# The tail of a hybrid encoder block: the last expert's down weights by columns, and the last norm's mean and offset added on PE

## The chip, the cores and the metric

The kernel runs on one core of one Trainium2 chip. The metric is the device time of one execution in microseconds (us), the median of three runs. TensorE is called PE, VectorE DVE, ScalarE ACT, GpSimd POOL, and SyncE, whose queue issues most DMAs, SP.

## The reference

One encoder layer over 256 tokens of width 1024 in float32: a projection, a sparse and a banded attention, a merge, a layer norm, and then the part that matters here, a mixture of 32 experts of which every token uses four, and a last layer norm.

```
for each expert e:   h = (clip(x @ w_up + b_up) + 1) * swish(min(x @ w_gate + b_gate, 7))
                     y = h @ w_down[e] + b_down[e]
ffn[t] = sum over the token's four experts of gate * y
z = alpha * x + ffn
out = (z - mean(z)) * rsqrt(var(z) + 1e-5) * ln2_g + ln2_b
```

## The kernel before

All 32 experts are run, each on up to 64 gathered tokens, so their weights are streamed once: per expert four loads of 2 MB ("gu", gate and up weights) and two of 2 MB ("d", down weights). A load goes into one of 13 slots of 2 MB; `plan` writes down the order (gate and up of expert e + 1, then down of expert e), `pump` issues on SP's queue as many loads as slots are free, and `take` hands a landed one to PE. SP works through its queue in program order, and a load waits there for an earlier one to land or for its slot.

The loop over experts has this order of the work: gate and up products of e on PE (`run_gate_up`, lines 782 and 784), the copy of the two results to the tile `work["gu"]` on ACT (`evac_gu`, through `acopy`, line 176), the down product of expert e - 1 (`run_down`, line 816) and its copy, and `act_fn`: transposes on PE (line 799), then some six DVE operations and one ACT operation for each half (lines 803 to 809). After every second expert `combine` (line 828) multiplies the down results by the routing weights and adds them to four PSUM banks, `sums[tb][n]` (two blocks of 128 tokens, two halves of 512 columns), which hold alpha * x from the start. At the end of iteration 26 the 32 down biases are loaded into the single tile "bd" (line 984), and at the end of iteration 28 they are added by PE. All order is written by hand: every engine does its instructions in the order of the program.

Behind the loop the last expert, 31, has a tail of its own. Its gate and up products are copied and activated, then expert 30's down product runs, then its own. Its down weights come as four pieces of 1 MB, by halves of the columns and halves of the contraction. `down_half` (line 1007) multiplies a piece in products of 256 columns, 64 partitions each, `combine_half` (line 1014) adds to the sums, and `bn_stats` (line 1016) reads each bank. The gain and offset of the last norm come in one row of 8 KB behind the last weights (line 994) and are spread to all partitions by POOL (line 995). The norm then runs per token block: block 0 on DVE, with two passes per half (subtract the mean and multiply by the gain, multiply by the inverse deviation and add the offset), block 1 with one ACT pass (line 1036) and two more on POOL or DVE. Each of the four results of 128 x 512 is stored by a DMA of its own (lines 1040 to 1047).

Of the kernel before, what the change touches and what calls it, by code (L numbers as in the profile page):

```python
# [20 lines left out]
CAP = 64  # L21
OVERFLOW_AT = 20
BD_AT = 26
TOPK = 64
ALPHA = 2.0 ** 0.25
EPS = 1e-5
# [25 lines left out]
def body(nc, tc, slots, sm, psp, xT_d, x_d, w_g0, w_qi, w_in, ikgb_d, wuk_d,  # L52
# [12 lines left out]
    def two(name):  # L65

        t = slot(name)
        return t[:, 0:2048], t[:, 2048:4096]

    def one(name):  # L70

        return slots[1].tile([128, 2048], F32, name=name, tag="one")
# [4 lines left out]
    def bank(name):  # L77
        return psp.tile([128, 512], F32, name=name, tag="ps")
# [4 lines left out]
    def plan(key, src):  # L83
        pending.append((key, src))
# [12 lines left out]
    def take(key):  # L97
        while key not in loaded:
            load_next()
        return loaded[key]  # L100

    def both(src, i):
        return lambda t: [(t[:, h * 2048:(h + 1) * 2048], src[i + h]) for h in range(2)]
# [11 lines left out]

    def plan_d(e):
        for c in range(2):

            plan(("d", e, c), wd_d[e, c] if e < NE - 1 else both(wdl_d, 2 * c))

    plan_gu(0)
    for e in range(NE):
# [49 lines left out]
    def vcopy(o, i):  # L172
        V.tensor_copy(o, i)

    def acopy(o, i):
        A.activation(o, i, AF.Copy)  # L176
# [643 lines left out]
    def rows_of(e, p, first=0, size=512):  # L820

        r = slice(64 * (e % 2), 64 * (e % 2) + 64)
        for n in range(2):
            acopy(work["y"][r, first + n * size:first + (n + 1) * size], p[64 * n:64 * n + 64, 0:size])
# [98 lines left out]
    def down_biases(bd_s):  # L923

        gT = bd_s[0:NE, 1024:1024 + T]
        bd = bd_s[0:NE, 0:1024]
        p = bank("gT")
        for tb in range(NT):
            PE.transpose(p[0:NE, tb * 128:(tb + 1) * 128], gt[:, tb, :], ident)
        acopy(gT, p[0:NE, 0:256])  # L930
        for tb in range(NT):
            for n in range(2):
                summed(tb, n, gT[:, tb * 128:(tb + 1) * 128], bd[:, n * 512:(n + 1) * 512])

    def count():

        p = bank("cnt")
        for tb in range(NT):
            PE.matmul(p[:, 0:NE], tri[:, 1, :], selb[:, tb, :], start=(tb == 0), stop=(tb == 1))
        V.tensor_reduce(cnt, p[:, 0:NE], axis=AX.X, op=ALU.max)  # L940
        V.tensor_copy(cnti, cnt)
# [14 lines left out]
    for e in range(last):  # L956
        ps = run_gate_up(e)
        if e == 0:
            for gain, op in ((ln1[0], ALU.mult), (ln1[1], ALU.add)):
                V.tensor_tensor(x1, x1, gain[:, None, :].to_broadcast([128, NT, D]), op=op)  # L960
            open_work()
            gates()
        evac_gu(ps)
        if e == 0:
            open_sums()
        if e == 1:
            dispatch_weights(0)
        if e == 3:
            count()
        if e >= 1:  # L970
            run_down(e - 1)
        else:
            pump(0)
        if e % 2 == 1:
            dispatch(e // 2 + 1)
            dispatch_weights(e // 2 + 1)
        act_fn(work["hT"], bias_of(0, e), bias_of(1, e))
        if e >= 2 and e % 2 == 0:
            combine(e // 2 - 1)
        if e == OVERFLOW_AT:  # L980
            overflow(one("ov"))
        if e == BD_AT:
            bd_s = one("bd")
            SP.dma_start(bd_s[0:NE, 0:1024], bd_d)
        if e == BD_AT + 2:
            down_biases(bd_s)

    evac_gu(run_gate_up(last))
    hT = xg_rows(0, 4).rearrange("p j (a s) -> p (j a) s", a=2)
    act_fn(hT, bias_of(0, last), bias_of(1, last))  # L990
    run_down(last - 1)
    ln2_s, acc_s = two("ln2_acc")
    acc = acc_s.rearrange("p (b c) -> p b c", b=2)
    SP.dma_start(ln2_s[0:1, :], ln2_d)
    G.partition_broadcast(ln2_s, ln2_s[0:1, :])
    A.preload_act_table(AF.Sqrt)


    lng, lnb = ln2_s[:, 0:1024], ln2_s[:, 1024:2048]
    hs = [slice(h * 512, (h + 1) * 512) for h in range(2)]  # L1000
    yps = [bank("y"), bank("y")]

    def down_half(h, c2, js=range(4)):
        wd = take(("d", last, h)).rearrange("p (j f) -> p j f", j=KD)
        for j in js:
            for n in range(2):
                PE.matmul(yps[h][64 * n:64 * n + 64, 0:256], hT[:, 4 * c2 + j, :], wd[:, 4 * c2 + j, n * 256:(n + 1) * 256],  # L1007
                          start=(c2 + j == 0), stop=(c2 == 1 and j == 3), skip_group_check=True)
        if c2 == 1 and 3 in js:
            rows_of(last, yps[h], h * 512, 256)  # L1010

    def combine_half(h, tbs=range(NT)):
        for tb in tbs:
            PE.matmul(sums[tb][h], work["pt"][:, last // 2 % 2, tb, :], work["y"][:, h * 512:(h + 1) * 512],  # L1014
                      start=False, stop=True, skip_group_check=True)
            V.bn_stats(lnst[:, tb, h, :], sums[tb][h])  # L1016
            if h == 1:
                V.bn_aggr(lnmv[:, tb, 0:2], lnst[:, tb, 0:2])  # L1018

    down_half(0, 0)  # L1020
    down_half(0, 1)
    down_half(1, 0)
    down_half(1, 1, (0, 1))
    combine_half(0, (0,))
    down_half(1, 1, (2, 3))
    combine_half(0, (1,))
    combine_half(1)
    A.activation(lnmv[:, :, 2], lnmv[:, :, 1], AF.Sqrt, bias=epst[:, 0:1])
    m0, m1 = lnmv[:, 0, :], lnmv[:, 1, :]
    a0, a1 = acc[:, 0, :], acc[:, 1, :]  # L1030
    s0, s1 = sums
    V.scalar_tensor_tensor(a0[:, hs[0]], s0[0], m0[:, 0:1], lng[:, hs[0]], op0=ALU.subtract, op1=ALU.mult)  # L1032
    V.reciprocal(lnmv[:, :, 3], lnmv[:, :, 2])
    V.tensor_scalar(m1[:, 4:5], m1[:, 0:1], m1[:, 3:4], -1.0, op0=ALU.mult, op1=ALU.mult)  # L1034
    for h in (1, 0):
        A.activation(a1[:, hs[h]], s1[h], AF.Identity, bias=m1[:, 4:5], scale=m1[:, 3:4])
    G.tensor_tensor(a1[:, hs[1]], a1[:, hs[1]], lng[:, hs[1]], op=ALU.mult)
    G.tensor_tensor(a1[:, hs[1]], a1[:, hs[1]], lnb[:, hs[1]], op=ALU.add)
    V.scalar_tensor_tensor(a0[:, hs[0]], a0[:, hs[0]], m0[:, 3:4], lnb[:, hs[0]], op0=ALU.mult, op1=ALU.add)  # L1039
    SP.dma_start(out_d[0:128, hs[0]], a0[:, hs[0]])  # L1040
    V.scalar_tensor_tensor(a0[:, hs[1]], s0[1], m0[:, 0:1], lng[:, hs[1]], op0=ALU.subtract, op1=ALU.mult)  # L1041
    V.scalar_tensor_tensor(a0[:, hs[1]], a0[:, hs[1]], m0[:, 3:4], lnb[:, hs[1]], op0=ALU.mult, op1=ALU.add)  # L1042
    SP.dma_start(out_d[0:128, hs[1]], a0[:, hs[1]])
    A.dma_start(out_d[128:256, hs[1]], a1[:, hs[1]])
    V.tensor_tensor(a1[:, hs[0]], a1[:, hs[0]], lng[:, hs[0]], op=ALU.mult)  # L1045
    V.tensor_tensor(a1[:, hs[0]], a1[:, hs[0]], lnb[:, hs[0]], op=ALU.add)  # L1046
    SP.dma_start(out_d[128:256, hs[0]], a1[:, hs[0]])


# [62 lines left out]
```

## Time and profile before

| what | us |
|---|---|
| median of 3 runs | 1116.69 (1115.77 to 1116.75) |
| the profiled execution | 1116.79 |
| its span, first to last instruction | 1114.9 |
| PE busy / DVE / ACT / POOL | 1033.9 / 310.1 / 232.6 / 25.4 |
| granted PE clock, mean | 0.996 |
| HBM read | 435.48 MB, 392 GB/s over the span |

The span is what the trace shows; the rest of the execution's time lies around it. A busy share says nothing about what bounds a stage: matmuls are pipelined, and PE is counted as busy while a product drains. What ended an idle time is given behind an arrow as its releaser.

### The profile page before, as it was taken

The page shows a single profiled execution, that of the slowest core. Times are in us where ns is not written, and L with a number is a line of the kernel's source. Part 1 is how long each engine was busy: PE and PEld are TensorE (multiplying, and loading weights), DVE is VectorE, ACT ScalarE, POOL GpSimd, SP SyncE. Part 2 cuts the span into 40 slices and gives each one's busy share as a digit, 9 for nine tenths or more (in the row PEclk, how much of TensorE's full clock was granted, in tenths as well). Part 3 has the DMA queues.
Part 4 walks back from the last instruction along what each step waited for, and adds up shares of the span by engine and source line. Part 5 has one row for each costly group of instructions (what it writes and reads, how often), then busy time and mean ns, then how long its engine had stood idle before and what let it go on. Part 6 is the DMA issues. An engine that isn't in the chain of part 4 may idle for free. (4 is left out here: it accounts for less than half of the span.)

```text
span 1114.9 us, 13223 instructions
## 1 busy us (share of the span) xinstructions
PE 1033.9 (93%) x5559; PEld 524.8 (47%) x5559; DVE 310.1 (28%) x743; ACT 232.6 (21%) x433; POOL 25.4 (2%) x23
## 2 busy tenths in 40 slices
PE   8999999999999999988889988897998888889995
PEld 8999998443434344333343434342434343333432
DVE  5879667411111111211111111111111102011123
ACT  3647534211111111111111111111111111111112
POOL 0320000000000000000000000000000000000001
PEclk9999999999999999999999999999999999999999
DMA  9926649999999999999999999999999999999993
GB/s 365 386 77 265 263 170 398 395 424 427 427 427 429 426 429 427 429 427 426 429 427 428 427 428 427 428 427 426 427 427 428 426 427 430 425 411 429 427 424 147
DMA packets 34678, 437.44 MB, mean 392 GB/s; under 512 B 4116, under 2 KB 4884, under 8 KB 6324
## 3 DMA queue, kind: packets, MB, share of 16 engines
q1 hardware_dynamic: 34182, 435.46, 92.9%
q10 hardware_dynamic: 432, 1.08, 0.3%
q8 instruction: 45, 0.74, 0.3%
q14 instruction: 19, 0.16, 0.0%
HBM read 435.48 MB, written 1.05 MB: 392 GB/s over the span
## 5 line engine op out<-in xcount | busy, mean ns | idle before, releaser
L782 PE MATMUL gu<-ld,x_wa 128*64 128x512 f32 x1024 | 452.1, 596 | 15.7 <-DMA ld<-in_dram 12.0
L784 PE MATMUL gu<-ld,x_wa 128*64 128x512 f32 x1024 | 452.1, 596 | 0.0
L782 PEld LDWEIGHTS gu<-ld,x_wa 128*64 128x64 f32 x1024 | 136.3, 137 | 309.6 <-issue 275.0
L816 PE MATMUL y<-ld,wb_wc 128*64 128x512 f32 x992 | 223.7, 595 | 49.0 <-DMA ld<-in_dram 49.0
L803 DVE TENSOR_TENSOR wb_wc<-tr,wb_wc 128x256 f32<-128x256 f32 x64 | 27.0, 422 | 688.6 <-PE tr L799 688.6
L816 PEld LDWEIGHTS y<-ld,wb_wc 128*64 128x64 f32 x992 | 75.9, 137 | 192.9 <-issue 186.0
L784 PEld LDWEIGHTS gu<-ld,x_wa 128*64 128x64 f32 x1024 | 136.3, 137 | 0.0
L176 ACT ACTIVATE wb_wc<-gu 128x512 f32<-128x512 f32 x64 | 38.2, 597 | 394.5 <-PE gu L784 394.5
L176 ACT ACTIVATE wb_wc<-y 64x512 f32<-64x512 f32 (+1 forms) x66 | 38.2, 578 | 256.8 <-PE y L816 250.2
L281 PE MATMUL fm<-xhl,halves 128*128 128x256 f32 x672 | 82.2, 284 | 0.0
L281 PEld LDWEIGHTS fm<-xhl,halves 128*128 128x128 f32 x672 | 81.1, 192 | 0.9 <-issue 0.5
L654 PEld LDWEIGHTS ga<-x_wa 128*128 128x128 f32 x512 | 61.8, 196 | 12.8 <-issue 12.8
L654 PE MATMUL ga<-x_wa 128*128 128x128 f32 x512 | 65.4, 285 | 0.2 <-DVE x_wa L648 0.2
L828 PE MATMUL sum<-wb_wc 128*128 128x512 f32 x120 | 54.0, 592 | 0.0
L176 ACT ACTIVATE halves<-ld 128x1024 fp32r<-128x1024 f32 x48 | 47.2, 1050 | 25.3 <-PE fm L281 10.0
L181 DVE TENSOR_TENSOR halves<-ld,halves 128x1024 fp32r<-128x1024 f32 x42 | 48.7, 1221 | 6.9 <-ACT halves L176 6.9
L805 ACT ACTIVATE x_wa<-wb_wc 128x256 f32<-128x256 f32 x64 | 26.6, 416 | 79.9 <-DVE wb_wc L804 77.1
L799 PEld LDWEIGHTS tr<-ident,wb_wc 128*128 128x128 f32 x256 | 33.3, 207 | 13.7 <-issue 12.6
L799 PE MATMUL tr<-ident,wb_wc 128*128 128x128 f32 x256 | 37.7, 290 | 0.0
L828 PEld LDWEIGHTS sum<-wb_wc 128*128 128x128 f32 x120 | 21.8, 192 | 21.5 <-issue 17.9
L809 DVE TENSOR_TENSOR wb_wc<-wb_wc,x_wa 128x256 f32<-128x256 f32 x62 | 26.4, 425 | 6.5
L808 DVE SCALAR_TENSOR_TENSOR wb_wc<-wb_wc 128x256 f32<-128x256 f32 x64 | 27.2, 426 | 2.2
(215 smaller groups left out, 591.0 us busy)
## 6 DMA issues: line engine op xcount, KB each, us to landing
ld<-in_dram SPq DMA_DIRECT2D x190, 2048.0 KB, 39.1
ld<-in_dram SPq DMA_DIRECT2D x28, 1024.0 KB, 13.0
wq<-in_dram SPq DMA_DIRECT2D x2, 512.0 KB, 7.5
wq<-in_dram SPq DMA_DIRECT2D x1, 1024.0 KB, 9.1
biasB<-in_dram SPq DMA_DIRECT2D x1, 1024.0 KB
x_wa<-in_dram SPq DMA_DIRECT2D x1, 1024.0 KB
out_dram<-ln_acc SPq DMA_DIRECT2D x3, 256.0 KB, 2.0
xT_g<-in_dram ACTq DMA_DIRECT2D x1, 600.0 KB, 5.7
```

The costliest lines, as they stand in the source:

```text
L176: A.activation(o, i, AF.Copy)
L181: sub.tensor_tensor(lo.bitcast(F32R), t, hi, op=ALU.subtract)
L281: PE.matmul(ps[j // 2][:, j % 2 * 256:j % 2 * 256 + 256], part(i, b, k, 4)[:, j * 128:(j + 1) * 128], xHL[a][:, 4 * c + k, :], start=(c + ...
L654: PE.matmul(ps[j // per][:, (j % per) * n:(j % per + 1) * n], x1_cols(tb, j), Pt, start=(tb == 0 and j % per == 0), stop=(tb == 1), skip_g ...
L782: PE.matmul(ps[n][0:64, :], xe(j), wg(j, cs), start=(j == 0), stop=(j == KD - 1), skip_group_check=True)
L784: PE.matmul(ps[n][64:128, :], xe(j), wu(j, cs), start=(j == 0), stop=(j == KD - 1), skip_group_check=True)
L799: PE.transpose(p[:, i * 128:(i + 1) * 128], gu[:, (j // 2) * 256 + j % 2:(j // 2) * 256 + 256:2], ident)
L803: V.tensor_tensor(gg, pv[:, :, 0, :], bg(js), op=ALU.add)
L805: A.activation(sg_, gg, AF.Sigmoid, scale=1.702)
L808: V.scalar_tensor_tensor(uu, uu, 1.0, gg, op0=ALU.add, op1=ALU.mult)
L816: PE.matmul(p[64 * n:64 * n + 64, :], hT[:, j, :], wd(j, slice(n * 512, (n + 1) * 512)), start=(j == 0), stop=(j == KD - 1), skip_group_ch ...
L828: PE.matmul(sums[tb][n], lhsT, rhs, start=start, stop=stop, skip_group_check=True)
```

## The change

The last expert's down weights are cut by columns alone. The first 512 columns are one load of 2 MB; the other 512 are three loads into one slot: 256 columns (1 MB), and the last 256 columns in two halves of the contraction (512 KB each). A new `down_cols` multiplies 512, 256 and 256 columns; its two output halves are copied by ACT and DVE side by side. `combine_cols` adds a column block to the sums and takes statistics of 256 columns at a time. A new `weigh` multiplies a column block of the sums by the gain on DVE and adds the result through a product with the identity on PE into new PSUM banks, `normed`.

The mean and the offset enter there too, as one product with a contraction of six rows: (rounded mean, rounded deviation, the rests of both, and the rounded pair once more) for each token against (-gain, offset, ...) for each column, in the one-pass format float32r with the gain and offset split into a rounded part and a rest. The columns `six` are made by three small DVE operations and two transposes on PE, the rows by a new `last_rows` on DVE. At the end one multiplication by the inverse deviation, on DVE for block 0 and on ACT for block 1, and four stores, all from SP.

The gain and offset are loaded at the end of iteration 29 (`LN2_AT`) by two DMAs, one row and six rows, into the single tile after the biases; at the end of iteration 30 POOL spreads the gain and DVE runs `last_rows`.

```diff
+LN2_AT = 29
-            plan(("d", e, c), wd_d[e, c] if e < NE - 1 else both(wdl_d, 2 * c))
+            plan(("d", e, c), wd_d[e, c] if e < NE - 1 else last_down(c))
+    def last_down(c):
+        if c == 0:
+            return wdl_d[0]
+        return lambda t: [(t[:, i:j], wdl_d[1][:, i:j]) for i, j in ((0, 2048), (2048, 3072), (3072, 4096))]
...
+    def last_rows(raw):
+        hi = work["gu"][0:6, :]
+        sgn, sel, other = [nm[0:6, 0, i:i + 1] for i in range(3)]
+        V.tensor_reduce(sgn, ident[0:6, 0:6:2], axis=AX.X, op=ALU.add)
+        V.tensor_scalar(sgn, sgn, -2.0, 1.0, op0=ALU.mult, op1=ALU.add)
+        V.tensor_reduce(sel, ident[0:6, 4:6], axis=AX.X, op=ALU.add)
+        V.tensor_scalar(other, sel, -1.0, 1.0, op0=ALU.mult, op1=ALU.add)
+        V.tensor_scalar(raw, raw, sgn, None, op0=ALU.mult)
+        vcopy(hi.bitcast(F32R), raw)
+        V.tensor_tensor(raw, raw, hi, op=ALU.subtract)
+        V.tensor_scalar(hi, hi, other, None, op0=ALU.mult)
+        V.scalar_tensor_tensor(raw, raw, sel, hi, op0=ALU.mult, op1=ALU.add)
...
+        if e == LN2_AT:
+            ln2_s = one("ln2")
+            lng, raw = ln2_s[:, 0:1024], ln2_s[0:6, 1024:2048]
+            SP.dma_start(lng[0:1, :], ln2_d[0:1, :])
+            SP.dma_start(raw, ln2_d)
+        if e == LN2_AT + 1:
+            G.partition_broadcast(lng, lng[0:1, :])
+            last_rows(raw)
     evac_gu(run_gate_up(last))
...
-    ln2_s, acc_s = two("ln2_acc")
-    SP.dma_start(ln2_s[0:1, :], ln2_d)
-    G.partition_broadcast(ln2_s, ln2_s[0:1, :])
+    acc = slot("acc")[:, 0:2048].rearrange("p (b c) -> p b c", b=2)
+    exact = slot("rows")
+    rows, cols = exact[0:6, 0:1024], exact[0:6, 1024:1280]
+    acopy(rows.bitcast(F32R), raw)
...
+    def down_cols(p, first, n, js):
+        wd = take(("d", last, first // 512))
+        base = 0 if first < 512 else (first - 512) * KD
+        wd = wd[:, base:base + KD * n].rearrange("p (j f) -> p j f", j=KD)
+        for j in js:
+            for h in range(2):
+                PE.matmul(p[64 * h:64 * h + 64, 0:n // 2], hT[:, j, :], wd[:, j, h * (n // 2):(h + 1) * (n // 2)],
+                          start=(j == 0), stop=(j == KD - 1), skip_group_check=True)
+        if KD - 1 in js:
+            r = slice(64, 128)
+            for h, copy in ((0, acopy), (1, vcopy)):
+                copy(work["y"][r, first + h * n // 2:first + (h + 1) * n // 2], p[64 * h:64 * h + 64, 0:n // 2])
+    def combine_cols(first, n, tb):
+        p = sums[tb][first // 512][:, first % 512:first % 512 + n]
+        PE.matmul(p, work["pt"][:, last // 2 % 2, tb, :], work["y"][:, first:first + n],
+                  start=False, stop=True, skip_group_check=True)
+        for i in range(first, first + n, 256):
+            V.bn_stats(st[:, tb, i // 256, :], sums[tb][i // 512][:, i % 512:i % 512 + 256])
+    def weigh(first, n, tb):
+        cs, o = slice(first, first + n), first % 512
+        V.tensor_tensor(acc[:, tb, cs], sums[tb][first // 512][:, o:o + n], lng[:, cs], op=ALU.mult)
+        if normed[tb][first // 512] is None:
+            normed[tb][first // 512] = bank("out")
+        PE.matmul(normed[tb][first // 512][:, o:o + n], ident, acc[:, tb, cs], start=(o == 0), stop=False,
+                  skip_group_check=True)
+    down_cols(yps[0], 0, 512, range(KD))
+    for tb in range(NT):
+        combine_cols(0, 512, tb)
+    down_cols(yps[1], 512, 256, range(KD))
+    for tb in range(NT):
+        weigh(0, 512, tb)
+    for tb in range(NT):
+        combine_cols(512, 256, tb)
+    yq = bank("y")
+    down_cols(yq, 768, 256, range(0, 4))
+    for tb in range(NT):
+        weigh(512, 256, tb)
+    down_cols(yq, 768, 256, range(4, 8))
+    for tb in range(NT):
+        combine_cols(768, 256, tb)
+        V.bn_aggr(lnmv[:, tb, 0:2], st[:, tb])
+    A.activation(lnmv[:, :, 1], lnmv[:, :, 1], AF.Sqrt, bias=epst[:, 0:1])
+    weigh(768, 256, 0)
+    V.tensor_copy(six[:, :, 0:2].bitcast(F32R), lnmv[:, :, 0:2])
+    V.tensor_tensor(six[:, :, 2:4], lnmv[:, :, 0:2], six[:, :, 0:2], op=ALU.subtract)
+    V.tensor_copy(six[:, :, 4:6], six[:, :, 0:2])
+    weigh(768, 256, 1)
+    p = bank("cols")
+    for tb in range(NT):
+        PE.transpose(p[0:6, tb * 128:(tb + 1) * 128], six[:, tb, :], ident)
+    acopy(cols.bitcast(F32R), p[0:6, 0:256])
+    V.reciprocal(lnmv[:, :, 3], lnmv[:, :, 1])
+    for h in range(2):
+        for tb in range(NT):
+            cs = slice(h * 512, (h + 1) * 512)
+            PE.matmul(normed[tb][h], cols[:, tb * 128:(tb + 1) * 128].bitcast(F32R), rows[:, cs].bitcast(F32R),
                       start=False, stop=True, skip_group_check=True)
...
+            o = acc[:, tb, cs]
+            if tb:
+                A.activation(o, normed[tb][h], AF.Copy, scale=lnmv[:, tb, 3:4])
+            else:
+                V.tensor_scalar(o, normed[tb][h], lnmv[:, tb, 3:4], None, op0=ALU.mult)
+            SP.dma_start(out_d[tb * 128:(tb + 1) * 128, cs], o)
```

The old `down_half`, `combine_half` and the norm's passes from line 1028 on are taken out.

## Rows read from the trace of the kernel before

**Rows 1.** The chain that ended last, 1000 to 1115 us: start us, us, what
```profile
1068.74 29.40 DMA ld<-in_dram
...
1098.19 1.08 PE y L1007 x8
...
1110.93 0.69 DVE ln_acc L1046
```

**Rows 2.** Timeline of SP's queue, 940 to 1115 us: start us, us, what, count
```profile
959.81 0.33 SPq L984 DMA_DIRECT2D bd<-in_dram  x1
964.68 104.39 SPq L90 DMA_DIRECT2D ld<-in_dram  x23
```

**Rows 3.** Timeline of the last expert's stage: idle time before, and its releaser, in brackets
```profile
1081.40 0.60 ACT L176 ACTIVATE wb_wc<-gu 128x512 f32<-128x512 f32 x1 [14.38 <-PE gu L784]
...
1082.92 0.42 DVE L803 TENSOR_TENSOR wb_wc<-tr,wb_wc 128x256 f32<-128x256 f32 x1 [14.77 <-PE tr L799]
...
1083.58 3.65 PE L816 MATMUL y<-ld,wb_wc 128*64 128x512 f32 x16
...
1088.43 3.65 PE L816 MATMUL y<-ld,wb_wc 128*64 128x512 f32 x16 [1.19 <-DMA ld<-in_dram]
...
1091.60 2.30 POOL L995 PARTITION_BROADCAST ln_acc<-ln_acc  x1 [888.31 <-DMA ln_acc<-in_dram]
1091.88 3.65 PE L1007 MATMUL y<-ld,x_wa 128*64 128x256 f32 x32
...
1093.32 1.28 ACT L996 ACT_TABLE_LOAD   x1
```

**Rows 4.** Windows at the stream's end: us, busy by engine (count), PEclk, DMA share, GB/s
```profile
1084.00:1085.00 1.00, 1.00 (x8) 0.37 (x6) 0.83 (x4) 0.18 (x1) 0.00 (x0) 1.00 1.01 426
1094.00:1095.00 1.00, 1.00 (x13) 0.79 (x10) 0.00 (x0) 0.60 (x1) 0.00 (x0) 1.00 0.60 254
1097.00:1098.00 1.00, 0.77 (x8) 0.27 (x4) 0.00 (x0) 0.00 (x0) 0.00 (x0) 1.00 0.06 25
```

**Rows 5.** DVE's groups by form, whole span: busy us, mean ns of one, idle before
```profile
L181 DVE TENSOR_TENSOR halves<-ld,halves 128x1024 fp32r<-128x1024 f32 x42 | 48.7, 1221 | 6.9 <-ACT halves L176 6.9
...
L807 DVE TENSOR_SCALAR wb_wc<-wb_wc 128x256 f32<-128x256 f32 x64 | 18.8, 294 | 2.2
...
L532 DVE TENSOR_TENSOR gates<-br,gates 128x512 f32<-128x512 f32 x8 | 5.5, 689 | 4.4 <-PE br L523 4.4
...
L557 DVE BATCH_NORM_STATS2 lnst<-x_wa 128x6 f32<-128x256 f32 x4 | 1.6, 421 | 0.1
...
L384 DVE TENSOR_SCALAR misc_qb<-misc_qb 128x384 f32<-128x384 f32 x1 | 0.4, 362 | 0.0
...
L562 DVE BATCH_NORM_AGGREGATE lnmv<-lnst 128x2 f32<-128x24 f32 x1 | 0.3, 263 | 0.0
```

**Rows 6.** ACT's groups by form, whole span, same columns
```profile
L176 ACT ACTIVATE wb_wc<-y 64x256 f32<-64x256 f32 x4 | 1.5, 377 | 6.0 <-PE y L1007 6.0
L1036 ACT ACTIVATE ln_acc<-sum,lnmv 128x512 f32<-128x512 f32 x2 | 1.4, 773 | 1.0 <-DVE lnmv L1034 1.0
...
L1028 ACT ACTIVATE lnmv<-lnmv,ikgb 128x2 f32<-128x2 f32 x1 | 0.3, 298 | 3.0 <-DVE lnmv L1018 3.0
```

**Rows 7.** PE's timeline at products 128 wide and at the old combine
```profile
132.81 2.84 PE L458 MATMUL pv<-pt,sa_vb 128*64 128x128 f32 x48
...
1101.28 2.92 PE L1014 MATMUL sum<-wb_wc 128*128 128x512 f32 x6
```

**Rows 8.** Windows of 1 us around a pause of PE at 771 us, columns as in rows 4
```profile
771.50:772.50 1.00, 0.00 (x0) 0.00 (x0) 0.20 (x1) 0.00 (x0) 0.00 (x0) 1.00 1.03 426
774.50:775.50 1.00, 0.93 (x4) 0.43 (x6) 0.29 (x2) 0.00 (x0) 0.00 (x0) 0.81 1.08 451
776.50:777.50 1.00, 1.00 (x5) 0.32 (x3) 0.00 (x0) 0.00 (x0) 0.00 (x0) 0.50 1.04 442
778.50:779.50 1.00, 1.00 (x8) 0.45 (x6) 0.00 (x0) 0.00 (x0) 0.00 (x0) 0.98 0.91 377
```

More of the change, by code (lines that the diff above doesn't have):

```diff
@@ L991, in body @@
     run_down(last - 1)
-    ln2_s, acc_s = two("ln2_acc")
-    acc = acc_s.rearrange("p (b c) -> p b c", b=2)
-    SP.dma_start(ln2_s[0:1, :], ln2_d)
-    G.partition_broadcast(ln2_s, ln2_s[0:1, :])
+    acc = slot("acc")[:, 0:2048].rearrange("p (b c) -> p b c", b=2)
+    exact = slot("rows")
+    rows, cols = exact[0:6, 0:1024], exact[0:6, 1024:1280]
+    acopy(rows.bitcast(F32R), raw)
     A.preload_act_table(AF.Sqrt)
-    lng, lnb = ln2_s[:, 0:1024], ln2_s[:, 1024:2048]
-    hs = [slice(h * 512, (h + 1) * 512) for h in range(2)]
+    six = pos[:, :, 0:6]
@@ L1001, in body @@
+    st = lnst
     yps = [bank("y"), bank("y")]
-    def down_half(h, c2, js=range(4)):
-        wd = take(("d", last, h)).rearrange("p (j f) -> p j f", j=KD)
-        for j in js:
[L1006 to L1010, printed above, removed]
@@ L1012, in combine_half @@
-    def combine_half(h, tbs=range(NT)):
-        for tb in tbs:
-            PE.matmul(sums[tb][h], work["pt"][:, last // 2 % 2, tb, :], work["y"][:, h * 512:(h + 1) * 512],
-                      start=False, stop=True, skip_group_check=True)
[L1016 to L1047, printed above, removed]
+    normed = [[None, None], [None, None]]
+    def down_cols(p, first, n, js):
+        wd = take(("d", last, first // 512))
+        base = 0 if first < 512 else (first - 512) * KD
+        wd = wd[:, base:base + KD * n].rearrange("p (j f) -> p j f", j=KD)
+        for j in js:
+            for h in range(2):
[5 more added lines that the diff above has]
+                copy(work["y"][r, first + h * n // 2:first + (h + 1) * n // 2], p[64 * h:64 * h + 64, 0:n // 2])
@@ L1072 @@
     bias = lambda b: b.reshape(NE, 4, 128, 2).transpose(2, 0, 1, 3).reshape(128, NE, KD)
+    wl = a["w_down"][0, NE - 1].reshape(4, 128, 2, D).transpose(1, 0, 2, 3).reshape(128, KD, D)
     pairs = lambda w: w.reshape(4, 128, 2, -1).transpose(1, 0, 2, 3).reshape(128, KD, -1)
@@ L1095 @@
         a["w_down"][0].reshape(NE, 2, 2, 128, 2048).transpose(0, 1, 3, 2, 4).reshape(NE, 2, 128, 4096),
-        a["w_down"][0, NE - 1].reshape(2, 2, 128, 2, 2, 512).transpose(4, 0, 2, 1, 3, 5).reshape(4, 128, 2048),
+        np.stack([np.concatenate([wl[:, :, o:o + n].reshape(128, -1) for o, n in cut], axis=1)
+                  for cut in (((0, 512),), ((512, 256), (768, 256)))]),
         a["b_down"][0],
-        np.concatenate([a["ln2_g"][0], a["ln2_b"][0]])[None, :],
+        np.stack([a["ln2_g"][0], a["ln2_b"][0]] * 3),
     ]
```

## The prediction

> **What bounds the kernel now.** I read the chain that ended last first. Up to 1098.19 us it is weights arriving: the last piece is issued at 1068.74 and takes 29.40 us to land [rows 1]. From there to the last DVE operation, which ends at 1111.62, the chain is PE and DVE work on the last expert and the final norm [rows 1], and 3.28 us more pass to the end of the span, the last store's landing among them. So the middle is bound by the DMA stream at 426 GB/s [rows 4], a load of 2 MB each 4.9 us (2.097 MB / 426 GB/s), and two things can change the time: when the last weights are there, and the 16.7 us of tail behind them.
>
> Then I read the stage before the tail in order of time [rows 3]. ACT copies the last expert's gate and up products out at 1081.40, DVE begins its activations at 1082.92 after 14.77 us with nothing to do, PE begins expert 30's down product at 1083.58 and waits 1.19 us for that expert's second weight load, until 1088.43. The last expert's down product starts at 1091.88. So PE has little over a microsecond to spare in this stage.
>
> **Part 1: where the new load of gain and offset stands.** SP issues in program order. The bias load at the end of expert 26 is followed by 23 weight loads before the old gain load [rows 2]. Counted back from the end these are four pieces for expert 31's down, then 2 + 4 + 2 + 4 + 2 + 4 loads of whole experts, and one: the bias load stood between the two down loads of expert 27. The new loads stand at the end of expert 29, three experts later, so between the two down loads of expert 30. The first of these lands 4.9 us before 1088.43, at 1083.5. SP's queue holds only the two small issues more, at turns that wait for a landing anyway. The rest of the order keeps its bytes, and 28 KB more cost under 0.1 us at 426 GB/s, so the last weights still land near 1098.3.
>
> DVE gets the nine operations of last_rows at the end of expert 30, and five of them need that load. They write and read the first six partitions of the tile "gu", so the ACT copy at 1081.40 must wait for them, and behind it stand, each on its engine, PE's transposes, DVE's activations and, in PE's order, expert 30's down product. When does the load land? The old one-row gain load was issued after the last piece and yet landed at 1091.60, 6.6 us ahead of it [rows 1, 3]. So a small load on few DMA engines can be early: of the 16, 0.60 were still busy at 1094.5 and 0.06 at 1097.5 [rows 4]. The bounds for the six rows are 1083.5 - 6.6 = 1076.9 and 1083.6. A transfer over six engines ends with its slowest, and more than half of the engines lag by 3 us or more; I take 1082.1, 1.4 us ahead of the slowest engine.
>
> The Trainium skill speaks to this in "DMA: Bandwidth & Descriptors" ("Why a DMA increments its semaphore by 16 and not by 1"; "Latency and other measured facts"): a load runs on as many engines, up to 16, as divide its rows, the lowest-numbered ones, and engines 7 and 15 usually lag. By it the six rows would miss the laggards and land early, which is rival B. The early one-row load agrees; that more than half of the engines lag does not look like two alone, and no row shows their numbers.
>
> The five operations over 1024 columns: three with one tensor operand at 0.70 (0.294 at 256 columns, 0.362 at 384, so 0.53 ns a column) [rows 5], two with two tensors at 1.22 [rows 5], with 0.04 between: 4.75 us. A POOL broadcast beside them could add 1; the one-row gain load of that broadcast lands earlier, so I leave it out. Then 1082.1 + 4.75 = 1086.9 for the ACT copy, 5.5 us late. From copy to down product took 2.18 us, so 1089.1.
>
> PE is then idle from 1082.2 to 1087.6. After a pause from about 771 to 774.5 the granted clock was 0.50 (1.2 GHz) until 778.5, some 3.9 us after work began again [rows 8]. I take the same here: 0.75 us more for the transposes and 0.8 us on the down product. That product has its weights by now and needs two stretches of 3.44 us (the row of 3.65 without its last drain [rows 3]): 1089.1 + 0.75 + 0.8 + 6.9 = 1097.6. This is S, the start of the last expert's down product, 5.7 us later than before.
>
> **Part 2: the first 512 columns as one load.** Two 1 MB loads become one of 2 MB. It lands 4.9 us before 1098.2, at 1093.3, so without Part 1 S would be 1093.3 and not 1091.88. With Part 1 nothing waits for a landing any more, and the quarter-sized last piece frees nobody.
>
> **Part 3: the tail from S.** I follow PE's order, in us after S. First block, same products as the 3.65 row: 3.65. ACT and DVE copy the two halves side by side, 0.38 [rows 6] and about 0.42 (the row for statistics of 256 columns [rows 5]), and the combine of 512 columns is two products of 0.86 (six records in 2.92, so 0.43 each and 0.34 to finish) [rows 7]; before, this copy lay under other products. PE is free at 6.0. ACT comes to its copy in time: ahead of it stand expert 30's two copies and the copy of the six rows (at most 0.77 for each 512 columns [rows 6]) and the table load (1.28 [rows 3]), 4.4 us at most and by shorter copies about 3.6; if the 3.65 us of products did not cover them, 0.7. The block of 256 columns has products 128 wide; nearest is the row of 48 in 2.84, 0.055 each [rows 7], so 32 take 1.95: 7.95. DVE's copy (0.3), its multiplication by the gain (0.69) [rows 5] and two identity products of 0.86: 10.8. Combine of 256 columns, two at 0.43: 11.7. Half of the last quarter, 0.88: 12.55. PE waits for DVE's statistics (0.42 each) [rows 5] and multiplications (0.43); the identity products end at 13.8. The other half quarter: 14.7. Copy and combine bring the first new statistics at 16.0; two of 0.42 and two aggregates of 0.26 [rows 5] end at 17.4, the square root (0.30) [rows 6] at 17.8. The three small operations for the six columns at about 0.2 and two multiplications of 0.43 share DVE until 18.9; identity product 19.4, two transposes 20.05, ACT's copy (0.38) [rows 6] 20.5, first six-row product 21.0. ACT then evicts two halves at 0.77 [rows 6], the second starting on the heels of the first: 22.85.
>
> Before, S to the last operation was 1111.62 - 1091.88 = 19.74, though it waited for three landings on the way. So the tail is 3.1 us longer: to the old PE work (3.65 a block twice, 3.4 of combining) come 3.4 us of identity products, two transposes and four six-row products, and the chain from the last statistics to the end (16.0 to 22.85, 6.9 us) is hardly shorter than the old one (1104.2 to 1111.6, 7.4 us). Four stores of 256 KB within 1.1 us add 0.25 (0.6 us each at 426 GB/s, less their spacing). What is removed (POOL's multiplication and addition, the six DVE passes, the late gain load) lay on the path only in the last 5 us, and is counted in the old 7.4.
>
> **Sum.** Span 1097.6 + 22.85 + 3.28 + 0.25 = 1124.0. The profiled execution took 1116.79 for a span of 1114.9, so 1.89 more: 1125.9; it was 0.10 over the median, so 1125.8, slower by 0.8%. About 0.2% (2.2 us) is what a measurement of this kernel can tell from no change.
>
> **Rivals.**
> B, the small load is early: if its six rows land by 1079.5, last_rows ends by 1084.2 and S is set by the 2 MB load at 1093.3. Then 1093.3 + 26.4 + 1.8 = 1121.5, slower by 0.4%. For it: the one-row load's 6.6 us. Against: six engines, not one.
> C, other side: the tail is fed by landings and not by PE. If all steps ahead of the last half quarter ran under the arriving weights, only 22.85 - 13.8 = 9.05 us would follow the last landing at 1098.3: span 1098.3 + 9.05 + 3.5 = 1110.9, time 1112.7, faster by 0.4%. The place is the 13.8 us between S and that half quarter; it decides for faster if they shrink below about 9 us and S is 1093.3. Only if identity and 128-wide products cost far less than the rows, and DVE's turns hid under them, could that be; the 0.86 and 0.055 speak against it.
> D, worse: load at the last engine to finish, POOL's broadcast beside last_rows, a longer stay at 1.2 GHz: 1128.5 and over.
> A', forecast without the fall of the clock: 1124.2.
>
> **How the numbers follow.** Forecast with A' 0.53 (own range 1123 to 1128), B 0.33, C 0.10, D 0.04. Unknown ends: load 1079.5 to 1083.6 moves the time by -4.3 to +1.5; 128-wide products up to 0.11 each (weight load bound) +3.5; tail overlaps -2. The range 1119.0 to 1128.5 leaves out C and D. Faster 0.05 and same 0.06 are C with a sliver of B; slower 0.89.
>
> **What would show it.** Right: DVE idle until about 1082 and then 4.75 us of last_rows; ACT's copy of "gu" waiting for DVE; PE idle some 5 us and a window at 0.50 after it; the last expert's product free of DMA waits; 23 us from its start to the last eviction. Wrong: last_rows done before 1081.4 (B); PE waiting for weights after 1097 (C); a 256-column block far from 1.95 us.

## The result, and the profile after

The changed kernel takes 1128.54 us (four runs, 1127.7 to 1130.59) where the kernel before, beside it, takes 1116.72: a ratio of 1.0107 [1.0095, 1.0119], so it is slower by 1.1%. Forecast were 1125.8, slower by 0.8%. The direction and the places were right; the time lies 2.7 us above the forecast and 0.04 us above the range's upper end. One of the eleven executions of experiment 7's kernel below took 3766.78 us; it is left out of that kernel's ratio, though not of its median in the table (1117.09 without it). The profiled execution of the change took 1128.26 us for a span of 1126.6, 11.7 us more than the span before, at a mean granted clock of 0.988 instead of 0.996.

I read the chain that ended last first, as before: start, us, what.

```profile
1053.56 29.26 DMA ln<-in_dram
1082.90 0.75 DVE ln L949
...
1087.79 0.60 ACT wb_wc L182
...
1090.42 8.66 PE y L822 x32
...
1103.44 1.98 PE sum L1051 x4
1105.43 1.92 PE y L1041 x32
...
1108.84 1.96 PE out L1062 x4
...
1120.85 1.32 ACT acc L1099 x2
```

In [rows 1] the chain is weights until 1098.19. Now the last transfer on it is not a weight at all: it is "ln", the 24 KB of gain and offset, from 1053.56 to 1082.82. Behind it stand DVE's last_rows, ACT's copy of "gu", expert 30's down product in one stretch of 32 and then the new tail, on PE nearly throughout.

The timeline shows the same stage with what each engine waited for in brackets; it answers to [rows 3].

```profile
1077.35 1.30 POOL L1013 PARTITION_BROADCAST ln<-ln  x1 [873.87 <-DMA ln<-in_dram]
...
1082.90 0.74 DVE L949 TENSOR_SCALAR ln<-ln,nm 6x1024 f32<-6x1024 f32 x1 [14.53 <-DMA ln<-in_dram]
...
1086.42 1.27 DVE L953 SCALAR_TENSOR_TENSOR ln<-ln,nm,wb_wc 6x1024 f32<-6x1024 f32 x1
1087.79 1.09 ACT L182 ACTIVATE wb_wc<-gu 128x512 f32<-128x512 f32 x2 [21.02 <-DVE ln L953]
1088.44 1.98 PE L805 MATMUL tr<-ident,wb_wc 128*128 128x128 f32 x8 [6.73 <-ACT wb_wc L182]
...
1090.35 8.70 PE L822 MATMUL y<-ld,wb_wc 128*64 128x512 f32 x32
...
1098.88 3.62 PE L1041 MATMUL y<-ld,x_wa 128*64 128x256 f32 x32
...
1102.55 0.38 ACT L182 ACTIVATE wb_wc<-y 64x256 f32<-64x256 f32 x1
1102.96 0.43 DVE L179 COPY wb_wc<-y 64x256 f32<-64x256 f32 x1 [8.65 <-ACT wb_wc L182]
...
1105.36 1.97 PE L1041 MATMUL y<-ld,x_wa 128*64 128x128 f32 x32
```

Read the brackets downwards. DVE waits 14.53 us for the six rows, ACT 21.02 us for DVE, PE 6.73 us for ACT: one late transfer of 24 KB stops three engines in turn. Not all of this is new: in the kernel before, DVE was idle for 14.77 us and ACT for 14.38 us at the same place [rows 3]. The delay is in what follows. The ACT copy that ran at 1081.40 before [rows 3] runs at 1087.79, 6.4 us later. PE's two products from 1090.35 have no DMA in a bracket: neither waited for its weights. And ACT and DVE, meant to copy side by side, copy one after the other.

Windows in the columns of [rows 4] show the clock after PE's pause.

```profile
1086.00:1087.00 1.00, 0.00 (x0) 0.00 (x0) 0.96 (x2) 0.00 (x0) 0.00 (x0) 0.91 0.97 410
1088.00:1089.00 1.00, 0.56 (x3) 0.57 (x4) 0.00 (x0) 0.87 (x2) 0.00 (x0) 0.50 0.92 389
1093.00:1094.00 1.00, 1.00 (x6) 0.34 (x4) 0.83 (x3) 0.18 (x1) 0.00 (x0) 0.68 0.55 229
1094.00:1095.00 1.00, 1.00 (x6) 0.28 (x4) 0.32 (x1) 0.00 (x0) 0.00 (x0) 1.00 0.55 225
```

The granted clock falls to 0.50 (1.2 GHz) near the end of the pause and stays there until about 1093.6, for 5.2 us of PE's work after it resumed at 1088.44.

The last view is SP's queue, for where the loads are issued; it answers to [rows 2].

```profile
1048.72 0.28 SPq L1010 DMA_DIRECT2D ln<-in_dram  x1
1053.56 0.28 SPq L1011 DMA_DIRECT2D ln<-in_dram  x1
1058.50 19.85 SPq L91 DMA_DIRECT2D ld<-in_dram  x5
1121.39 1.82 SPq L1102 DMA_DIRECT2D out_dram<-acc  x4
```

Two small issues, then the last five weight issues, then the four stores within 1.82 us. From the end of the last eviction (1120.85 + 1.32 = 1122.17) to the end of the span pass 4.43 us, where 3.28 passed before. The rate in the DMA view from 1120 to 1127 us, in 40 slices, shows the stores as one block without a gap:

```profile
GB/s 0 0 0 0 0 0 0 0 0 0 0 0 82 351 374 374 386 363 398 386 386 340 410 398 351 398 398 398 199 0 0 0 0 0 0 0 0 0 0 0
```

So the 11.7 us of the span lie in three places: the last down product starts 7.0 us later (1098.88 against 1091.88 [rows 3]), from there to the last operation it takes 23.29 instead of 19.74 (+3.55), and the way to the end is 1.15 longer.

### The profile page after: what moved, and what is told of

It reads as the page before. It is cut to its first block, busy times and chain, and to the rows that moved or that the text cites. A ratio compares the mean times of both kernels' runs of the same rounds, so it can differ in the third digit from the quotient of the medians.

```text
span 1126.6 us, 13348 instructions
## 1 busy us (share of the span) xinstructions
PE 1044.1 (93%) x5613; PEld 528.4 (47%) x5613; DVE 314.8 (28%) x763; ACT 233.1 (21%) x434; POOL 21.8 (2%) x21
## 3 DMA queue, kind: packets, MB, share of 16 engines
HBM read 435.50 MB, written 1.05 MB: 387 GB/s over the span
## 4 chain that ended last, share of the span: by engine, by line
DMA 62%; PE 34%; DVE 2%; ACT 1%; issue 1%; SPq 0%; ACTq 0%; DVEq 0%
DMA ld<-in_dram 59%; PE gu L788 10%; PE fm L287 7%; PE y L822 5%; DMA ln<-in_dram 3%; PE br L529 2%; PE ga L660 1%; PE sum L834 1%; PE tm L272 1%; PE wo L680 1%; PE tr L805 1%; PE sce L333 1%; PE qi L258 1%; DMA xT_g<-in_dram 0%; PE pv L464 0%
## 5 line engine op out<-in xcount | busy, mean ns | idle before, releaser
L182 ACT ACTIVATE wb_wc<-y 64x512 f32<-64x512 f32 (+2 forms) x65 | 37.6, 578 | 258.2 <-PE y L822 246.0
```

## The experiments

The question is what the three parts are made of: the wait for six rows, the fall of the clock, the new cut of the columns and the new ending. Each kernel was timed against the kernel before on the same chip; its median there stands beside.

| kernel | us | before, beside it | ratio [95%] | difference |
|---|---|---|---|---|
| the change | 1128.54 | 1116.72 | 1.0107 [1.0095, 1.0119] | +11.8 |
| 1: last_rows later | 1123.24 | 1117.18 | 1.0054 [1.0037, 1.0071] | +6.1 |
| 2: the wait alone, on before | 1123.0 | 1117.18 | 1.0047 [1.003, 1.0064] | +5.8 |
| 3: 1 and two 1 MB loads | 1121.74 | 1117.18 | 1.0046 [1.0029, 1.0062] | +4.6 |
| 4: 3 without identity products | 1117.26 | 1117.08 | 1.0004 [0.9994, 1.0013] | +0.2 |
| 5: the change, PE kept busy | 1126.46 | 1117.18 | 1.0084 [1.0067, 1.0101] | +9.3 |
| 6: column cut with the old ending | 1118.5 | 1117.08 | 1.0013 [1.0003, 1.0022] | +1.4 |
| 7: 3 in another order | 1117.19 | 1117.08 | 1.0 [0.999, 1.0009] | +0.1 |
| 8: 7 with another column cut | 1115.28 | 1116.98 | 0.9983 [0.9974, 0.9992] | -1.7 |

**Experiment 1** takes the wait away and nothing else: DVE's last_rows moves behind the activation of the last expert, so that ACT's copy of "gu" is no longer queued behind it.

```diff
         if e == LN2_AT + 1:
             G.partition_broadcast(lng, lng[0:1, :])
-            last_rows(raw)
...
     act_fn(hT, bias_of(0, last), bias_of(1, last))
+    last_rows(raw)
     run_down(last - 1)
```

> last_rows stands behind the last expert's activations in DVE's order, all else as in the changed kernel. Theory (wait and tail): the wait for the six-row load costs the start of the last expert's down product 5.6 us (1098.88 against the landing of its first 2 MB at about 1093.3), and the rest of the loss is the longer tail. The product then starts at 1093.3 and the time falls from 1128.5 to about 1122.9. Rival 1 (tail alone: the wait is made up for later): 1127 to 1128.5. Rival 2 (wait alone: the tail is no longer than the old one): 1117 to 1119.

Measured: 1123.24. The timeline:

```profile
1080.70 0.60 ACT L182 ACTIVATE wb_wc<-gu 128x512 f32<-128x512 f32 x1 [14.41 <-PE gu L790]
...
1092.71 3.67 PE L1041 MATMUL y<-ld,x_wa 128*64 128x256 f32 x32 [1.26 <-DMA ld<-in_dram]
```

ACT's copy waits for PE's gate and up products again, as in [rows 3], and the last down product starts at 1092.71, 6.2 us earlier than in the change; it now waits 1.26 us for the single load of 2 MB. So the wait is half of the loss: 6.2 us at this place, 5.8 in the time. Some of it is lost again further down, as windows of the same kernel show:

```profile
1111.00:1112.00 1.00, 0.29 (x1) 0.29 (x2) 0.84 (x5) 0.30 (x1) 0.00 (x0) 0.96 0.00 0
1112.00:1113.00 1.00, 1.00 (x3) 0.48 (x3) 0.59 (x4) 0.00 (x0) 0.00 (x0) 0.50 0.00 0
```

PE is idle for about half of 1108 to 1112, and most of the last identity products, the transposes and the six-row products run at 0.50. In the change the clock falls only at 1121, under the last two six-row products.

**Experiment 2** is the reverse: the kernel before, with its old tail, gets the six-row load and last_rows at the same places as in the change. Its old load of gain and offset stays.

```diff
+LN2_AT = 29
...
+        if e == LN2_AT:
+            raw = one("ln2")[0:6, 1024:2048]
+            SP.dma_start(raw, ln2_d)
+        if e == LN2_AT + 1:
+            last_rows(raw)
```

> The kernel before with the six-row load and last_rows of the changed one added at the same places, and its old tail; the rows that they make are not used. Theory (wait and tail): the old tail starts at about 1098.9 in place of 1091.9 and has no more landings to wait for (0.7 us), so 1116.7 + 7.0 - 0.7 = 1123.0, with a PE clock of 0.50 after the wait. Rival 1 (the wait is made up for later): 1116.7 to 1118.

Measured: 1123.0, 5.8 us more than before. Its timeline:

```profile
1083.89 0.74 DVE L944 TENSOR_SCALAR ln<-ln,nm 6x1024 f32<-6x1024 f32 x1 [14.53 <-DMA ln<-in_dram]
...
1088.78 1.09 ACT L177 ACTIVATE wb_wc<-gu 128x512 f32<-128x512 f32 x2 [21.02 <-DVE ln L948]
...
1092.02 2.30 POOL L1015 PARTITION_BROADCAST ln_acc<-ln_acc  x1 [888.44 <-DVE wb_wc L808]
1092.04 2.42 DVE L809 SCALAR_TENSOR_TENSOR wb_wc<-wb_wc 128x256 f32<-128x256 f32 x1
...
1100.12 6.21 PE L1027 MATMUL y<-ld,x_wa 128*64 128x256 f32 x56
```

The same chain of waits, put on the old kernel, costs the same as taking it out of the new one gave back: 5.8 from both sides, and the time is the expected one. The parts behind it differ from what was expected. In the profiled execution (span 1121.8) the last down product starts 8.24 us later than in the kernel before, not 7.0, because the rows landed 1.0 us later still; its tail, which then waits for no landing, is shorter by 1.3 us, not 0.7. One row was not expected: a DVE operation that takes 0.42 elsewhere took 2.42 while POOL's broadcast ran beside it; the forecast had put 1 us on such a meeting. It did not move PE here: expert 30's down product was still running when DVE was done.

**Experiment 3** adds to experiment 1 that the first 512 columns come as two loads of 1 MB again.

```diff
         if c == 0:
-            return wdl_d[0]
+            return lambda t: [(t[:, i:i + 2048], wdl_d[0][:, i:i + 2048]) for i in (0, 2048)]
```

> As e1_rows_later, and the first 512 columns come as two loads of 1 MB, by halves of the contraction. Theory (PE sets the tail from its first product on): the product starts at 1091.9 in place of 1093.3 and the time falls by 1.4 us against e1_rows_later, to about 1121.5. Rival (landings of the later pieces set the tail): no change, 1122.9.

Measured: 1121.74, 1.5 us under experiment 1; their intervals overlap, but the spans (1121.5 and 1119.7) say the same. Of the 1.8 us between the spans the earlier start of the last down product is 0.74, which is the price of the single load; the rest, about 1.1, is that the clock holds here until 1113.6 (the window from 1113 to 1114 is at 0.80), by which time only the six-row products are left. So the 1.4 us that were expected came out, but only half of them in the expected way. The timeline has the last down product at the place of the kernel before (1091.88 [rows 3]), without a wait:

```profile
1091.97 3.65 PE L1041 MATMUL y<-ld,x_wa 128*64 128x256 f32 x32
```

What is left, 4.6 us, is all behind this product. The chain shows the identity products (L1062) on it three times:

```profile
1101.95 1.96 PE out L1062 x4
...
1105.79 1.06 PE out L1062 x4
...
1111.81 0.70 PE out L1062 x2
...
1114.98 0.69 ACT acc L1099
```

**Experiment 4** takes these products out of experiment 3; the multiplications by the gain stay on DVE. The output then lacks the gained sums and holds the six-row product alone.

```diff
-        PE.matmul(normed[tb][first // 512][:, o:o + n], ident, acc[:, tb, cs], start=(o == 0), stop=False,
-                  skip_group_check=True)
...
-                      start=False, stop=True, skip_group_check=True)
+                      start=True, stop=True, skip_group_check=True)
```

> As e3_two_loads, without the identity products: the sums times the gain are not added, so the output lacks them. Theory (the identity products lie on PE's path): 2.6 us less before the combine of the second block, 1.1 less between the halves of the last quarter, some 0.1 at the end, so 1121.7 - 3.8 = 1117.9. Rival (they hide under DVE's statistics and multiplications): 1121 or more.

Measured: 1117.26, no different from before. So the identity products, on PE's path as placed, cost 4.4 us; 3.72 of it (1.96 + 1.06 + 0.70) stands as their own time in the chain of experiment 3. If anything 4.4 is too little: the clock falls before the six-row products here, which take 2.07 us, and only under them in experiment 3, where they take 1.75. In the chain of experiment 4 the last eviction starts at 1110.79, 4.2 us earlier:

```profile
1110.79 0.69 ACT acc L1097
```

The stores do not change with it: from the end of this eviction (1111.48) to the end of the span (1115.5) pass 4.0 us, as in experiment 3, where the kernel before took 3.28.

**Experiment 5** leaves the change as it is and gives PE 100 small products to do during the wait, to keep its clock up.

```diff
     evac_gu(run_gate_up(last))
+    warm(100)
```

> The changed kernel with 100 small bf16 products on PE, results unused, in the wait for ACT's copy of the last gate and up products. Theory (the fall of the clock is part of the wait's price): no window at 0.50 after the wait; expert 30's down product takes 6.9 in place of 8.5 us and the transposes 0.75 less; time 1128.5 - 2.4 = 1126.1. Rival (PE has slack there, DVE's activations set the start): 1128.5.

Measured: 1126.46, 2.1 us under the change's median, and 2.5 if each is taken against the kernel before beside it. A window of it and its timeline:

```profile
1090.00:1091.00 1.00, 1.00 (x8) 0.41 (x6) 0.91 (x3) 0.37 (x1) 0.00 (x0) 1.00 0.88 369
```

```profile
1081.34 5.76 PE L232 MATMUL warm<-wt 128*128 128x128 bf16 x100
...
1088.33 1.23 PE L805 MATMUL tr<-ident,wb_wc 128*128 128x128 f32 x8 [1.24 <-ACT wb_wc L182]
...
1089.50 7.09 PE L822 MATMUL y<-ld,wb_wc 128*64 128x512 f32 x32
...
1096.41 3.62 PE L1042 MATMUL y<-ld,x_wa 128*64 128x256 f32 x32
```

The wait is still there (ACT's copy of "gu" starts at 1087.68), but the clock is 1.00 behind it. The eight transposes take 1.23 instead of 1.98 and the down product 7.09 instead of 8.70: 0.75 + 1.61 = 2.36 us for the fall of the clock, and the last down product starts 2.47 earlier.

**Experiment 6** keeps experiment 3's cut by columns and gives it the old ending: the old gain load, no identity or six-row products, the old passes of the norm.

```diff
-        if e == LN2_AT:
-            ln2_s = one("ln2")
...
-    last_rows(raw)
...
+    SP.dma_start(ln2_s[0:1, :], ln2_d[0:2, :].rearrange("(o r) d -> o (r d)", o=1))
...
-        weigh(0, 512, tb)
...
+    V.scalar_tensor_tensor(a0[:, hs[0]], s0[0], m0[:, 0:1], lng[:, hs[0]], op0=ALU.subtract, op1=ALU.mult)
...
+        A.activation(a1[:, hs[h]], s1[h], AF.Identity, bias=m1[:, 4:5], scale=m1[:, 3:4])
```

> As e3_two_loads with the old norm passes and the old gain load in place of the six rows, the identity products and last_rows; the column cut alone. Theory (the column cut costs little, the identity products carry the tail's loss): last statistics at about 1106.8, then the old passes as before, 6.5 us to the last operation, 3.3 to the end: 1118.5. Rival (the column cut carries the loss): over 1120.

Measured: 1118.5, so the cut by columns alone costs 1.4 us (0.3 to 2.5 by its interval). Against experiment 4 (+0.2) the six-row ending, were its identity products free, would be about 1.2 us shorter than the old one, stores included. The chain of experiment 6 ends in the old passes; DVE operations on 512 columns that take about 0.7 alone [rows 5] take 1.42 and 1.68 there, while POOL does its two. This part the new ending has done away with.

```profile
1109.79 1.42 DVE ln_acc L1085
1111.22 1.68 DVE ln_acc L1088
```

**Experiment 7** asks whether experiment 3's identity products can be hidden. PE does both first blocks before any combining and the last quarter in one go; the identity products stand behind the last combine, where PE would wait for statistics; ACT copies both halves, and the last store is issued by ACT. `weigh` is split for it into `gained`, DVE's multiplication, and `added`, the identity product.

```diff
     down_cols(yps[0], 0, 512, range(KD))
+    down_cols(yps[1], 512, 256, range(KD))
     for tb in range(NT):
         combine_cols(0, 512, tb)
-    down_cols(yps[1], 512, 256, range(KD))
     for tb in range(NT):
-        weigh(0, 512, tb)
+        gained(0, 512, tb)
+    down_cols(yq, 768, 256, range(KD))
...
+    for first, n in ((0, 512), (512, 256)):
+        for tb in range(NT):
+            added(first, n, tb)
```

> As e3_two_loads in another order: PE multiplies the second block before the first combine and the whole last quarter in one go, the identity products stand behind the last combine, beside the statistics, and before the six-row products; both output halves are copied by ACT; the last store is issued from ACT. Theory (what costs is PE's order and the turns between PE and DVE, not the ending): last combine at about 1102.7, last eviction at about 1108.5, time about 1114, below the kernel before. Rival (the ending costs what it costs wherever it stands): 1117 to 1119.

Measured: 1117.19, the time of before, 3 us more than was expected. The timeline says where they went:

```profile
1104.09 1.10 PE L1051 MATMUL sum<-wb_wc 128*128 128x256 f32 x4 [0.94 <-DVE acc L1059]
...
1105.03 3.17 PE L1066 MATMUL out<-acc,ident 128*128 128x512 f32 x10
1108.04 0.38 PE L1097 MATMUL cols<-ident,pos 128*6 128x128 f32 x2
...
1109.65 1.26 ACT L1107 ACTIVATE acc<-out,lnmv 128x512 f32<-128x512 f32 x2 [0.81 <-PE out L1103]
```

The last combine waits 0.94 us for DVE's multiplication, which reads other columns of the same bank, and the transposes of the six columns, which the end waits for, stand in PE's queue behind 3.17 us of identity products.

**Experiment 8** mends these two. The first block holds columns 0 to 255 and 512 to 767, the second 256 to 511, the third 768 to 1023, so that a combine and a multiplication meet less often in one bank, and the transposes stand ahead of the last two identity products.

```diff
-        np.stack([np.concatenate([wl[:, :, o:o + n].reshape(128, -1) for o, n in cut], axis=1)
-                  for cut in (((0, 512),), ((512, 256), (768, 256)))]),
+        np.stack([np.concatenate([wl[:, :, o].reshape(128, -1) for o in cut], axis=1)
+                  for cut in ((np.r_[0:256, 512:768],), (np.r_[256:512], np.r_[768:1024]))]),
...
+    down_block(yps[0], 0, 0, 512, (0, 512))
+    down_block(yps[1], 1, 0, 256, (256, 384))
...
+    for tb in range(NT):
+        gained(768, tb)
+    V.reciprocal(lnmv[:, :, 3], lnmv[:, :, 1])
+    added(768, 0)
+    finished(0)
+    added(768, 1)
+    finished(1)
```

> As e7_order with another cut of the columns, so that the last quarter's combine adds to a bank that DVE is done with: first block columns 0 to 255 and 512 to 767, then 256 to 511, then 768 to 1023; the transposes stand ahead of the last identity products. Theory (e7_order lost 1.0 us where the last combine waited for DVE's reads of the same bank and 1.1 us where the transposes stood behind the identity products): last combine at 1103.4 in place of 1104.1 for its first product, transposes at 1106 in place of 1108, last eviction at about 1109, time 1115.3. Rival (DVE's eight statistics and its multiplications, 6.2 us, are the bound there whatever the order): 1116.5 to 1117.2.

Measured: 1115.28 against 1116.98, a ratio of 0.9983 [0.9974, 0.9992]. This is the one version that is faster than both kernels, by 0.17%; the interval keeps clear of 1, but the gain is under the 0.2% that I named as what a measurement can tell, so it is at the edge of what these runs show. Its timeline:

```profile
1101.82 1.99 PE L1047 MATMUL sum<-wb_wc 128*128 128x256 f32 x8
...
1103.65 2.75 PE L1061 MATMUL out<-acc,ident 128*128 128x256 f32 x12
1106.24 0.38 PE L1103 MATMUL cols<-ident,pos 128*6 128x128 f32 x2
...
1109.14 0.69 ACT L1071 ACTIVATE acc<-out,lnmv 128x512 f32<-128x512 f32 x1 [0.60 <-PE out L1067]
```

The last combine has no bracket, most identity products lie at 1103.65, beside DVE's statistics and multiplications, and the transposes come 1.8 us earlier than in experiment 7. A third difference came with these two: the first 512 columns get their six-row products before the last identity product runs, and are evicted beside it. What each of the three is worth no run tells apart. The last eviction ends at 1109.83, where the last operation of before ended at 1111.62.

## Why the prediction was right in its places and short in its sizes

**The direction and the steps held.** The loads stand in SP's order where they were counted to be. The six rows landed at 1082.82 (forecast 1082.1), last_rows took 4.8 us (4.75), and ACT's copy of "gu" came at 1087.79 (1086.9). PE paused, its clock fell, no product after it waited for weights, and a block of 256 columns took 1.97 us (1.95). Experiments 1 and 2 show the wait as a cause from both sides, at 5.8 us; the forecast moved the start of the last down product by 5.7.

**The sizes that failed.** The sum came to a span of 1124.0 and the trace shows 1126.6. The step that failed is the size of three of its terms, the price of the low clock and of the late rows ahead of the last down product, the copies in the tail, and the stores; they make the 2.6 us.

- Start of the last down product: 1098.88, not 1097.6 (+1.3). The landing, taken "1.4 us ahead of the slowest engine", was 0.7 us later, and from it to ACT's copy passed 0.2 more than the sum has. Of "0.75 us more for the transposes and 0.8 us on the down product" the first was exact and the second was 1.61 by experiment 5. I had gone by [rows 8], where the clock is back 3.9 us after work began again, after a pause of 3.7 us, and where the first window is at 0.81; here, after a pause of 6.7 us, the clock was at 0.50 from the start of the work and stayed there for 5.2 us of it. Against these stands 0.4 us that the two ACT copies, now both ready at once, ran closer together than in [rows 3].
- The tail, from there to the last eviction: 23.29, not 22.85 (+0.4). "ACT and DVE copy the two halves side by side" did not happen. DVE's copy at 1102.96 waited for ACT's copy of 0.38, and in the two later blocks for one of 0.27. That is more than the whole excess, because two errors cancel here. The first new statistics came 17.3 us after the start of the last down product, not 16.0 (+1.3), of which these three waits are 0.9; from there to the last eviction passed 5.97, not 6.85 (-0.9). The forecast called that last stretch "hardly shorter than the old one" because it counted the old one from the second of the last two statistics; from the first, at 1103.37, it is 8.25 us, so the new ending is 2.3 us shorter. That the tail came out nearly right was luck. The lines of the first of these statistics, before and after:

```profile
1103.37 0.71 DVE lnst L1016
...
1116.20 0.44 DVE lnst L1054
```

- From the last eviction to the end of the span: 4.43, not 3.53 (+0.9). "Four stores of 256 KB within 1.1 us add 0.25" was the step. In the change they were issued over 1.82 us and added 1.15; at the 340 to 410 GB/s of the DMA view 1.05 MB need some 2.8 us (an estimate from that view), and the last store ends when all have been written.

The rest of the way to the median (0.1 us) is what lies around the span and the scatter of the runs. The forecast's own range ended at 1128, and 1128.5 is where rival D begins; that three small terms would err to the same side was not in it.

**The parts, in the runs' terms.** The 7.0 us before the last down product are the wait, 6.2 by experiment 1 (2.4 of it the clock, by experiment 5), and 0.74 for the single load of 2 MB, by experiment 3; the forecast had 5.7 for both. The 3.55 of the tail is about what the identity products cost: 3.4 us of them were named as the tail's main addition, 3.72 stand on the chain of experiment 3, and without them the tail of experiment 4 is as long as the old one (19.44 against 19.74). The 1.15 behind it is not theirs but the stores': the way from the last eviction to the end is 4.0 in experiments 3 and 4 alike, and 3.3 in experiment 6 with the old stores. Beside these the cut costs 1.4 and the six-row ending, stores included, gives about as much back. In the times the parts do not add up to the tenth, since the clock's fall in the tail comes and goes with them.

**The rivals.** B, the six rows early, fell: they landed at 1082.82, when it needed 1079.5. The one row, issued 4.84 us ahead of them and next to them in SP's queue, had landed by 1077.35: what spoke for B, an early load of one row, held again. The trace also records the single packets. Of the seven rows of 4 KB the first five ended between 1076.59 and 1078.36, and the last two at 1080.99 and 1082.16; in every other run with these two loads, too, two of the seven end after 1080.5. In experiment 2, where the six rows came alone, they ended from 1075.76 to 1083.06. So most rows of one load were as early as B wanted, and the slowest two made the load late, as the forecast had argued. By the rule of the Trainium skill that I had weighed ("DMA: Bandwidth & Descriptors", "Why a DMA increments its semaphore by 16 and not by 1" and "Latency and other measured facts") a load of six rows rides on the lowest-numbered engines and so misses the usual laggards 7 and 15. The early landing that follows from it did not come: the trace does not agree here, and the measurement decides. No row shows the engines' numbers. A', no fall of the clock, fell by the windows and by experiment 5. C, a tail fed by landings, fell: nothing waited for weights in the change's tail. Its condition, 13.8 us of work shrinking under the arriving weights, is what experiments 7 and 8 went after; with the wait gone and the identity products mostly hidden, 8 ends on its side, but by 1.7 us and not 4. D's price, 1128.5, is where the time came out, but only in part by its own mishaps: the rows landed half way to its bound and the stay at 1.2 GHz was longer, as it said; POOL's broadcast ran at 1077.35, clear of last_rows, and the copies and the stores were not in it.

**Left open.** Which DMA engines lag, and whether the six rows would land early if they were spread over other engines or cut into one-row loads, was not tried. Whether DVE's copy waits for ACT's because of the bank that both read or the tile that both write is not told apart by a run.

## What to carry to other kernels

A small load that is issued early in a full queue is not there early: find the instruction that first needs it, and what stands behind that one on its engine, before placing either; here moving one call a few lines down was worth 5.8 us. Work that is moved from DVE to PE is free only where PE waits: the identity products cost 4.4 us between the column blocks, and put behind the last combine, with a better cut, they came in a kernel that was 1.7 us faster than the one before, a gain at the edge of what a measurement can tell. And several terms that are each a few tenths too small add up on a long tail, so a range should let them err together.

## What the runs showed of the hardware that was not expected

- Two small loads that follow each other in one queue, with no other load between them, landed 5.5 us apart, the one row by 1077.35 and the six rows at 1082.82. They were issued 4.84 us apart, but the issue is not the reason: the packets of the six rows, all of one issue, themselves ended at least 5.4 us apart (7.3 us in experiment 2), and the load landed 0.7 us after its slowest row.
- After a pause of 6.7 us PE ran at 0.50 for 5.2 us of work. A hundred small products in the pause kept the clock at 1.00 and gave 2.1 to 2.5 us back.
- The clock also fell inside the tail where PE waited often: in experiment 1 to 0.50 from 1112, which cost it about 1.1 us against experiment 3, where it held until 1113.6.
- A DVE operation on 128x256 took 2.42 us instead of 0.42 while POOL's broadcast ran (experiment 2).
- Four stores of 256 KB, issued over 1.82 us, made the way from the last operation to the end of the span 4.43 us instead of 3.28.
